# Turning q, k, v and the head output on VectorE and through DRAM scratch in place of TensorE

## The chip, the cores and the metric

The kernel runs on one core of a Trainium2 chip. The metric is the device time of one execution in microseconds (us), as the median of several executions. The engines named below are PE (TensorE, with its weight load PEld), DVE (VectorE), ACT (ScalarE), POOL (GpSimd) and SP (SyncE, which here issues nearly all DMAs).

## The reference

One layer of a hybrid decoder for a prompt of 1024 tokens (D_MODEL 1024, 8 heads of 128) and for 8 single tokens with stored states. Branch A is a gated delta rule, branch B a conformer convolution; both go through gates and an output projection, and a convolutional feed-forward layer follows. What the change touches is in branch A:

```python
qkv_c = jax.nn.silu(causal_dwconv(qkv, s_qkv, conv_qkv_w))
q, k = l2norm(q), l2norm(k)                       # per head, over 128 channels
...
def step(s, xc):                                   # scan over chunks, per head
    qg_c, kg_c, u_c, w_c, qk_c, gl_c = xc
    v_new = u_c - jnp.einsum('bhck,bhkv->bhcv', w_c, s)
    o = jnp.einsum('bhck,bhkv->bhcv', qg_c, s) + jnp.einsum('bhij,bhjv->bhiv', qk_c, v_new)
    s = s * gl_c[..., None, None] + jnp.einsum('bhck,bhcv->bhkv', kg_c, v_new)
    return s, o
...
o = o * lax.rsqrt(jnp.mean(o * o, axis=-1, keepdims=True) + NORM_EPS) * delta_norm_w
o = o * jax.nn.silu(z)
y_a = o.reshape(b, t, V_DIM) @ w_o_delta
```

All of it is float32. The kernel reaches that by splitting each operand of a large product into a high and a low part and running three products (`gemm`, line 187).

## The kernel before

The input projection is a sequence of weight tiles of 128 output columns. Each weight tile is multiplied with the activations in three column tiles of 344 tokens; `gemm` issues 24 products of 128x344 for one of them, into one of two PSUM buffers `mm`. Raw weights come by SP into `wraw` (two buffers, line 144), ACT casts them to `whi` (L145), DVE or POOL makes `wlo` (L146). Per head there are tiles for k, q, v (`qkv_tile`: ACT evicts, DVE adds the short convolution with three `scalar_tensor_tensor`), for z, and gate and conformer tiles between them. The outputs `kT`, `qT`, `vT`, `zT` hold channels on partitions and 1024 tokens along the row.

The head work runs in the gaps of these products. It is written as Python generators that `tick` (L157) advances once in four products of a gemm (L189); `yield n` lets 2n ticks pass. The order of PE is exactly the order in which the program writes it (`manual_schedule`, L89). DVE, ACT, POOL and SP each have an order that a list scheduler set when the kernel was built; on the chip each engine runs its own list in order and waits where an operand is missing. A head's stages are:

- `delta_a` (L638): products of k with itself, their masks, and the solve of 32x32 blocks on DVE, with two small turns through DRAM (`d_a` to `ab`, `d_x` to `dt`, L688 to L711).
- `delta_q` (L716): products of k with q, and the sums of squares of q per token. For these `sumsq` (L626) turns q with eight 128x128 PE transposes (L631), and ACT squares the PSUM tiles (L635).
- `delta_b` (L740): v and k are turned in the same way (L753), and ACT scales them into `vs` and `kt` (L756). Then the blocks of the solve are merged: DVE puts `dt` into `xs` (L770, a 32x32 stream transpose), PE begins with the products of L773. Then comes the chain over 8 chunks of 128 tokens (L814 to L842). One step is: PE `pk` (L817), DVE `vs` (L82), PE `pv` (L822), ACT `vn` (L825), PE `po` (L828), PE `psS` (L831), DVE `S` (L82, or L837 in the first step), PE `po` again (L838), ACT twice into `oo` (L840, L841). The PSUM tags of `pk`/`pv`, `po` and `psS` have one buffer each.
- `delta_c` (L847): ACT scales `oo` per token (L860); in four quarters PE turns two chunks (L867) and DVE multiplies with `dnw` and `zT` back into `oo` (shown as L82, since `stt` is a helper). SP stores `oo` to `d_og` (L875), from which the heads come back as `og` later. The last head skips the store and is split in place into `oghi`/`oglo`, which the product with `wod` reads next.

`oo`, `kt`, `vs`, `zT` have one buffer each, so the chain of head h+1 can write its first `oo` (L840) only when head h's `oo` is stored (L875). In parallel DVE works off the depthwise convolution of the conformer (`cacc`, 240 instructions of 128x512).

Of the kernel before, what the change touches and what calls it, by code (L numbers as in the profile page):

```python
# [8 lines left out]
F32 = mybir.dt.float32  # L9
F32R = mybir.dt.float32r  # L10
I32 = mybir.dt.int32
AF = mybir.ActivationFunctionType
ALU = mybir.AluOpType
# [3 lines left out]
P = 128  # L17
D = 1024
KT = D // P
T = 1024  # L20
# [4 lines left out]
NH = 8  # L25
NC = T // P
HB = 32
# [39 lines left out]
def body(tc, I, O):  # L67
    nc = tc.nc
# [9 lines left out]
    def sub(out, a, b):  # L78
        nc.vector.tensor_tensor(out=out, in0=a, in1=b, op=ALU.subtract)  # L79

    def stt(out, a, s, b, op0, op1):
        nc.vector.scalar_tensor_tensor(out=out, in0=a, scalar=s, in1=b, op0=op0, op1=op1)  # L82

    def split(hi, lo, x):
        nc.scalar.copy(hi, x)  # L85
        sub(lo, x, hi.bitcast(F32))

    with top:
        top.enter_context(tc.manual_schedule(engines={mybir.EngineType.PE}))  # L89
        dram = top.enter_context(tc.tile_pool(name="dram", bufs=1, space=DRAM))  # L90
# [7 lines left out]
        ident = const[:, C_ID:C_ID + P]  # L98
# [9 lines left out]
        def rsqrt(out, x, pool, shape, iters=3):  # L108
            t = pool.tile(shape, F32, tag="rs_t", name="rs_t")
            nc.vector.tensor_scalar(out=out.bitcast(I32), in0=x.bitcast(I32), scalar1=-0.5, scalar2=MAGIC,  # L110
                                    op0=ALU.mult, op1=ALU.add)
            for _ in range(iters):
                mul(t, out, out)
                stt(t, t, -0.5, x, ALU.mult, ALU.mult)
                stt(out, t, 1.5, out, ALU.add, ALU.mult)
# [116 lines left out]
        dnw = cp.tile([P, 1], F32, name="dnw")  # L232
# [28 lines left out]
        hp = hstk.enter_context(tc.tile_pool(name="hp", bufs=1, side="right", **R))  # L261
# [8 lines left out]
        def trp():  # L270
            return pst.tile([P, 512], F32, tag="tr", name="tr")
# [351 lines left out]

        cs = [slice(c * P, (c + 1) * P) for c in range(NC)]

        def sumsq(src, ss):  # L626
            for half in range(2):
                g = trp()
                gv = g.rearrange("p (c i) -> p c i", i=P)
                for i in range(4):  # L630
                    nc.tensor.transpose(gv[:, i, :], src[:, cs[half * 4 + i]], ident)  # L631
                for i in range(4):
                    c = half * 4 + i
                    jk = hp.tile([P, P], F32, tag="jk", name="jk")
                    nc.scalar.activation(jk, gv[:, i, :], AF.Square, accum_out=ss[:, c:c + 1])  # L635
                yield 2

        def delta_a(X):  # L638
            h, kT = X["h"], X["kT"]
# [76 lines left out]
        def delta_q(X):  # L716
            h, kT, qT = X["h"], X["kT"], X["qT"]
            while "sc" not in X:
                yield
            pt = X["pt"]  # L720
            brk, c1, nc1g, rqs = X["sc"]
            gr2 = hp.tile([P, NC, P], F32, tag="gr", name="gr2")
            nc.sync.dma_start(gr2.rearrange("p c i -> p (c i)"),
                              d_gc[1, h * NC:(h + 1) * NC].rearrange("c i -> (c i)").unsqueeze(0).broadcast_to([P, T]))
            yield 3
            for half in range(2):
                g = trp()
                gv = g.rearrange("p (c i) -> p c i", i=P)
                for i in range(4):
                    c = half * 4 + i  # L730
                    nc.tensor.matmul(gv[:, i, :], kT[:, cs[c]], qT[:, cs[c]], start=True, stop=True)  # L731
                mul(pt[:, 4 * half:4 * half + 4, :], gv, pt[:, 4 * half:4 * half + 4, :])
                yield
            ss = hp.tile([P, NC], F32, tag="ss", name="ss")
            yield from sumsq(qT, ss)
            nc.vector.tensor_scalar(out=rqs, in0=ss, scalar1=EPS, scalar2=EPS / QS ** 2, op0=ALU.add, op1=ALU.mult)
            mul(qT, qT, gr2.rearrange("p c i -> p (c i)"))
            X.update(qdone=True)

        def delta_b(X):  # L740
            h, kT, qT, vT = X["h"], X["kT"], X["qT"], X["vT"]
# [4 lines left out]
            kt = hp.tile([P, NC, P], F32, tag="kt", name="kt")  # L746
            vs = hp.tile([P, NC, P], F32, tag="vs", name="vs")
            for src, dst, scl in ((vT, vs, brk), (kT, kt, eg[:, h, :])):
                for half in range(2):
                    g = trp()  # L750
                    gv = g.rearrange("p (c i) -> p c i", i=P)
                    for i in range(4):
                        nc.tensor.transpose(gv[:, i, :], src[:, cs[half * 4 + i]], ident)  # L753
                    for i in range(4):
                        c = half * 4 + i
                        nc.scalar.activation(dst[:, c, :], gv[:, i, :], AF.Copy, scale=scl[:, c:c + 1])  # L756
                    yield
                X["vt"] = True
            while "dt" not in X:
                yield  # L760
# [5 lines left out]
            zv = zp[:, 0:256].rearrange("p (c i) -> p c i", i=HB)  # L766
# [12 lines left out]
            tv = tp_[:, 0:256].rearrange("p (c i) -> p c i", i=HB)  # L779
# [32 lines left out]
            oo = hp.tile([P, NC, P], F32, tag="oo", name="oo")  # L812
# [30 lines left out]
            nc.sync.dma_start(O["dp"][:, h, :], S)  # L843
            X.update(oo=oo, ms=ms, chained=True)
            X["fin"] = spawn(delta_c(X))

        def delta_c(X):  # L847
            h, oo, ms, rqs = X["h"], X["oo"], X["ms"], X["sc"][3]
            while h == NH - 1 and oglo[h] is None:
                yield  # L850
            f = hp.tile([P, NC], F32, tag="f", name="f", bufs=2)
            x = hp.tile([P, NC], F32, tag="fx", name="fx")
            stt(x, ms, 1.0 / P, rqs, ALU.mult, ALU.add)
            rsqrt(f, x, hp, [P, NC])
            yield 6
            while "zT" not in X:
                yield
            zT = X["zT"]
            for c in range(NC):
                nc.scalar.activation(oo[:, c, :], oo[:, c, :], AF.Copy, scale=f[:, c:c + 1])  # L860
            yield 2
            for qr in range(4):
                g = trp()[:, 0:256]
                gv = g.rearrange("p (c i) -> p c i", i=P)
                for i in range(2):
                    c = qr * 2 + i
                    nc.tensor.transpose(gv[:, i, :], oo[:, c, :], ident)  # L867
                og = oo[:, 2 * qr:2 * qr + 2, :].rearrange("p c i -> p (c i)")
                sl = slice(256 * qr, 256 * qr + 256)
                stt(og, g, dnw, zT[:, sl], ALU.mult, ALU.mult)  # L870
                if h == NH - 1:
                    split(oghi[h][:, sl], oglo[h][:, sl], og)
                yield
            if h < NH - 1:
                nc.sync.dma_start(d_og[h], oo.rearrange("p c i -> p (c i)"))  # L875
            X["done"] = True
# [74 lines left out]
        oghi, oglo = [None] * NH, [None] * NH  # L951
# [32 lines left out]
        def chain_b():  # L984
            for h in range(NH):
                while len(Xs) <= h:
                    yield
                yield from delta_b(Xs[h])
# [128 lines left out]
        for m in range(KT):  # L1117
            w = next_w()
            for t, (t0, n, npr) in enumerate(th):
                sg = sgp.tile([P, TH], F32, tag="sg", name="sgb")  # L1120
                nc.sync.dma_start(sg, d_gb[m, :, t0:t0 + TH])
                g, bufs = sas[(NTH * m + t) % 4]
# [169 lines left out]
        for b in range(2):  # L1292
            X[b] = xpool[b].tile([P, KT, HB2], F32, name=f"x{b}")
            for m in range(KT):
# [13 lines left out]
                for j in range(2):  # L1308
                    sl = slice(j * Q, j * Q + Q)
# [419 lines left out]
```

## Time and profile before

| what | value |
|---|---|
| median of 3 executions | 1832.4 us (1830.82 to 1833.6) |
| the profiled execution | 1833.88 us, its span 1832.1 us |
| mean granted TensorE clock | 0.995 of full speed |
| busy: PE / PEld | 1792.0 us (98%) / 1769.3 us (97%) |
| busy: DVE / ACT / POOL | 1377.5 us (75%) / 892.7 us (49%) / 127.7 us (7%) |
| DMA queue of SP | 37.0% of 16 engines' span |

Busy time counts the instructions of an engine; PE's products are pipelined, so the distance of two starts, and not the duration of one, tells what an instruction adds. Heads 0 to 7 occupy 60 to 870 us of the span, about 91 us for each; output projection and feed-forward follow and are not touched by the change.

### The profile page before, as it was taken

How to read it: one execution, taken by the hardware profiler on the slowest of the kernel's cores; microseconds unless marked ns; L12 is line 12 of the kernel's file. 1: busy time of each engine (PE TensorE's matmuls, PEld its weight loads, DVE VectorE, ACT ScalarE, POOL GpSimd, SP SyncE). 2: the span in 40 equal slices, each digit the busy share in tenths (PEclk: the TensorE clock that was granted, in tenths of full speed). 3: DMA queues.
4: the chain of work that ended last, by engine and by line, in shares of the span. 5: the costliest groups of instructions: out<-in, count | busy, mean ns of one | idle time of the engine just before them, and what ended most of it. 6: DMA issues, size and time to landing. Idle time of an engine off the chain costs nothing.

```text
span 1832.1 us, 35468 instructions
## 1 busy us (share of the span) xinstructions
PE 1792.0 (98%) x13331; PEld 1769.3 (97%) x13331; DVE 1377.5 (75%) x3266; ACT 892.7 (49%) x2112; POOL 127.7 (7%) x249
## 2 busy tenths in 40 slices
PE   7899999999999999999999998999999999999997
PEld 6899999999999999999999998999999999999997
DVE  7998799689967996745438488987888788856553
ACT  5565466455655555554213344544444445544332
POOL 4410010001000100000000000100000000000000
PEclk9999999999999999999999999999999999999998
DMA  4143323222323233334657632322222224867562
GB/s 165 55 137 99 92 73 114 88 85 82 115 86 86 81 122 99 105 135 131 191 158 223 224 127 93 103 70 92 73 79 75 87 76 150 259 204 215 168 185 85
DMA packets 150988, 223.83 MB, mean 122 GB/s; under 512 B 37984, under 2 KB 86432, under 8 KB 150816
## 3 DMA queue, kind: packets, MB, share of 16 engines
q1 hardware_dynamic: 143760, 213.10, 37.0%
q10 hardware_dynamic: 7056, 8.47, 1.3%
q8 instruction: 104, 1.70, 0.4%
q14 instruction: 68, 0.56, 0.1%
HBM read 172.36 MB, written 49.14 MB: 121 GB/s over the span
## 4 chain that ended last, share of the span: by engine, by line
PE 91%; DVE 5%; DMA 2%; ACT 1%; issue 1%; SPq 0%; DVEq 0%; ACTq 0%
PE mm L187 44%; PE mm L1333 23%; PE mm L1598 13%; PE psS L831 1%; PE tr L666 1%; PE tr L731 1%; PE tr L753 1%; PE po L838 1%; PE pv L822 1%; PE po L828 1%; PE pk L817 1%; DVE xt L82 1%; PE tr L794 0%; PE tr L804 0%; PE tr L908 0%
## 5 line engine op out<-in xcount | busy, mean ns | idle before, releaser
L187 PE MATMUL mm<-hhi,whi 128*128 128x344 f32 x1360 | 449.3, 330 | 12.4 <-ACT whi L85 6.9
L187 PE MATMUL mm<-hhi,wlo 128*128 128x344 f32 x1360 | 448.4, 330 | 2.5 <-DVE wlo L79 2.4
L187 PE MATMUL mm<-hlo,whi 128*128 128x344 f32 x1360 | 438.5, 328 | 0.0
L187 PEld LDWEIGHTS mm<-hhi,whi 128*128 128x128 f32 x1360 | 258.4, 190 | 16.5 <-ACT whi L85 7.3
L187 PEld LDWEIGHTS mm<-hhi,wlo 128*128 128x128 f32 x1360 | 258.5, 190 | 4.8 <-DVE wlo L79 3.7
L187 PEld LDWEIGHTS mm<-hlo,whi 128*128 128x128 f32 x1360 | 254.9, 188 | 0.5
L1333 PE MATMUL mm<-l_t,uhi 128*128 128x258 f32 x704 | 200.3, 285 | 1.4 <-DVE l_t L79 1.4
L1333 PE MATMUL mm<-h_t,uhi 128*128 128x258 f32 x704 | 200.4, 285 | 0.0
L1333 PE MATMUL mm<-h_t,ulo 128*128 128x258 f32 x704 | 199.3, 283 | 0.0
L82 DVE SCALAR_TENSOR_TENSOR cacc<-u,ccw,cacc 128x512 f32<-128x512 f32 x240 | 172.6, 742 | 1.0 <-ACT cacc L570 0.9
L1598 PE MATMUL mm<-yl,wdh 128*128 128x344 f32 x528 | 169.5, 321 | 0.0
L1598 PE MATMUL mm<-yh,wdh 128*128 128x344 f32 x528 | 169.5, 321 | 0.0
L1598 PE MATMUL mm<-yh,wdl 128*128 128x344 f32 x528 | 169.3, 321 | 0.0
L79 DVE TENSOR_TENSOR wdl<-draw,wdh 128x512 fp32r<-128x512 f32 x144 | 91.9, 645 | 82.2 <-ACT wdh L85 80.6
L145 ACT CAST whi<-wraw 128x512 fp32r<-128x512 f32 x164 | 96.5, 628 | 100.9 <-PE mm L187 82.8
L85 ACT CAST wdh<-draw 128x512 fp32r<-128x512 f32 x144 | 82.9, 584 | 114.9 <-PE mm L1598 99.6
L1333 PEld LDWEIGHTS mm<-l_t,uhi 128*128 128x128 f32 x704 | 133.8, 190 | 2.2 <-DVE l_t L79 2.2
L1333 PEld LDWEIGHTS mm<-h_t,uhi 128*128 128x128 f32 x704 | 133.7, 190 | 0.5 <-ACT h_t L1190 0.2
L1333 PEld LDWEIGHTS mm<-h_t,ulo 128*128 128x128 f32 x704 | 133.5, 190 | 0.0
L187 PE MATMUL mm<-og,whi 128*128 128x344 f32 x512 | 123.1, 321 | 0.0
L146 DVE TENSOR_TENSOR wlo<-wraw,whi 128x512 fp32r<-128x512 f32 x160 | 107.9, 689 | 14.7 <-ACT whi L145 12.1
L85 ACT CAST uhi<-s 128x512 fp32r<-128x512 f32 x92 | 56.9, 621 | 105.3 <-PE mm L1333 101.4
(358 smaller groups left out, 4228.8 us busy)
## 6 DMA issues: line engine op xcount, KB each, us to landing
draw<-in_wdn SPq DMA_DIRECT2D x120, 256.0 KB, 2.8
raw<-in_wup SPq DMA_DIRECT2D x92, 256.0 KB, 2.7
yl<-d_y SPq DMA_DIRECT2D x21, 516.0 KB, 6.0
d_y<-av SPq DMA_DIRECT2D x21, 512.0 KB, 3.2
gr<-d_gc SPq DMA_DIRECT2D x16, 512.0 KB, 3.4
wraw<-in_wout SPq DMA_DIRECT2D x32, 256.0 KB, 2.8
xt<-in_xT SPq DMA_DIRECT2D x12, 344.0 KB, 6.7
d_ga<-sg ACTq DMA_DIRECT2D x24, 172.0 KB, 2.4
```

Source lines behind the costliest of these rows:

```text
L79: nc.vector.tensor_tensor(out=out, in0=a, in1=b, op=ALU.subtract)
L82: nc.vector.scalar_tensor_tensor(out=out, in0=a, scalar=s, in1=b, op0=op0, op1=op1)
L85: nc.scalar.copy(hi, x)
L145: nc.scalar.copy(hi[:, k:k + 4], raw)
L146: weng["e"].tensor_tensor(out=lo[:, k:k + 4], in0=raw, in1=hi[:, k:k + 4].bitcast(F32), op=ALU.subtract)
L187: nc.tensor.matmul(ps, lhs[:, k, :], r(k), start=k == 0 and i == 0, stop=k == kt - 1 and i == 2)
L666: nc.tensor.matmul(gv[:, i, :], kT[:, cs[c]], kT[:, cs[c]], start=True, stop=True)
L731: nc.tensor.matmul(gv[:, i, :], kT[:, cs[c]], qT[:, cs[c]], start=True, stop=True)
L753: nc.tensor.transpose(gv[:, i, :], src[:, cs[half * 4 + i]], ident)
L817: nc.tensor.matmul(pk, kT[:, cs[c]], S, start=True, stop=True)
L1333: nc.tensor.matmul(z[:, b, 0:Q], w[:, k, :], r[b][nm][:, k, :], start=start and n == 0, stop=n == 3 * KH - 1, skip_group_check=True)
L1598: nc.tensor.matmul(ps, w[:, f % KH, :], y[:, f % 3, :], start=h == 0 and n == 0, stop=h == 1 and n == 3 * (NF - 3 * KH) - 1)
```

## The change

A helper `flip` turns a 128x1024 tile: DVE transposes its 32x32 blocks in one STREAM_TRANSPOSE into `ty`, SP stores `ty` to DRAM scratch `d_t` (512 KB, two buffers), and four SP loads of 128 KB each bring it back with the blocks in their transposed places, into `tv`. `ty` and `tv` have the same tag with one buffer, so the load overwrites what was stored, and the next flip begins when the readers of `tv` are done. Each head has four flips: q for `sumsq`, v and k in `delta_b`, `oo` in `delta_c`. ACT and DVE read `tv` in SBUF where they read PSUM before. The waits between the stages, in ticks, change with it: 3 in place of 2 and 2 for q, 2 and 2 in place of 1, 1, 1, 1 for v and k, 2 and 1 in place of four times 1 for `oo`.

```diff
--- before.py
+++ after.py
@@ -623,17 +623,24 @@
 
         cs = [slice(c * P, (c + 1) * P) for c in range(NC)]
 
+        def flip(src):
+            ty = hp.tile([P, T], F32, tag="ty", name="ty")
+            d_t = dram.tile([P, T], F32, tag="d_t", name="d_t", bufs=2)
+            nc.vector.transpose(out=ty, in_=src.rearrange("p (c b r) -> p b c r", b=4, r=HB))
+            nc.sync.dma_start(d_t, ty)
+            tv = hp.tile([P, T], F32, tag="ty", name="tv")
+            dv = d_t.rearrange("(a r) (b x) -> b r a x", r=HB, b=4)
+            for b in range(4):
+                nc.sync.dma_start(tv[HB * b:HB * (b + 1)].rearrange("p (a x) -> p a x", a=4), dv[b])
+            return tv.rearrange("p (a c s) -> p c a s", a=4, c=NC)
+
         def sumsq(src, ss):
-            for half in range(2):
-                g = trp()
-                gv = g.rearrange("p (c i) -> p c i", i=P)
-                for i in range(4):
-                    nc.tensor.transpose(gv[:, i, :], src[:, cs[half * 4 + i]], ident)
-                for i in range(4):
-                    c = half * 4 + i
-                    jk = hp.tile([P, P], F32, tag="jk", name="jk")
-                    nc.scalar.activation(jk, gv[:, i, :], AF.Square, accum_out=ss[:, c:c + 1])
-                yield 2
+            tv = flip(src)
+            yield 3
+            for c in range(NC):
+                jk = hp.tile([P, P], F32, tag="jk", name="jk")
+                nc.scalar.activation(jk.rearrange("p (a s) -> p a s", a=4), tv[:, c], AF.Square,
+                                     accum_out=ss[:, c:c + 1])
 
         def delta_a(X):
             h, kT = X["h"], X["kT"]
@@ -746,15 +753,11 @@
             kt = hp.tile([P, NC, P], F32, tag="kt", name="kt")
             vs = hp.tile([P, NC, P], F32, tag="vs", name="vs")
             for src, dst, scl in ((vT, vs, brk), (kT, kt, eg[:, h, :])):
-                for half in range(2):
-                    g = trp()
-                    gv = g.rearrange("p (c i) -> p c i", i=P)
-                    for i in range(4):
-                        nc.tensor.transpose(gv[:, i, :], src[:, cs[half * 4 + i]], ident)
-                    for i in range(4):
-                        c = half * 4 + i
-                        nc.scalar.activation(dst[:, c, :], gv[:, i, :], AF.Copy, scale=scl[:, c:c + 1])
-                    yield
+                tv = flip(src)
+                yield 2
+                for c in range(NC):
+                    nc.scalar.activation(dst[:, c, :].rearrange("p (a s) -> p a s", a=4), tv[:, c], AF.Copy,
+                                         scale=scl[:, c:c + 1])
                 X["vt"] = True
             while "dt" not in X:
                 yield
@@ -859,18 +862,16 @@
             for c in range(NC):
                 nc.scalar.activation(oo[:, c, :], oo[:, c, :], AF.Copy, scale=f[:, c:c + 1])
             yield 2
-            for qr in range(4):
-                g = trp()[:, 0:256]
-                gv = g.rearrange("p (c i) -> p c i", i=P)
-                for i in range(2):
-                    c = qr * 2 + i
-                    nc.tensor.transpose(gv[:, i, :], oo[:, c, :], ident)
-                og = oo[:, 2 * qr:2 * qr + 2, :].rearrange("p c i -> p (c i)")
-                sl = slice(256 * qr, 256 * qr + 256)
-                stt(og, g, dnw, zT[:, sl], ALU.mult, ALU.mult)
-                if h == NH - 1:
-                    split(oghi[h][:, sl], oglo[h][:, sl], og)
-                yield
+            tv = flip(oo.rearrange("p c i -> p (c i)"))
+            yield 2
+            zv, ov = zT.rearrange("p (c b r) -> p b c r", b=4, r=HB), oo.rearrange("p c (b r) -> p b c r", b=4)
+            for b in range(4):
+                stt(ov[:, b], tv[:, :, b], dnw, zv[:, b], ALU.mult, ALU.mult)
+            if h == NH - 1:
+                og = oo.rearrange("p c i -> p (c i)")
+                for o in (0, 512):
+                    split(oghi[h][:, o:o + 512], oglo[h][:, o:o + 512], og[:, o:o + 512])
+            yield
             if h < NH - 1:
                 nc.sync.dma_start(d_og[h], oo.rearrange("p c i -> p (c i)"))
             X["done"] = True
```

The change adds 32 STREAM_TRANSPOSE to DVE, takes the 256 transposes from PE (11336 rows to 11255 with their grouping), and takes SP from 540 to 622 rows. The rest of PE's products keep their order.

How the lists move, at two places. First DVE around the beginning of the chain of head 1. `S<-psS` is the state after its first chunk, the next `vs<-` and `S<-S` are the second chunk's steps, `cacc` the conformer's convolution, `oo<-` the end of head 0. Before:

```order
L82 SCALAR_TENSOR_TENSOR oo<-tr,dnw,zT 128x256
L73 TENSOR_TENSOR prd<-stq,cqw 128x32
L82 SCALAR_TENSOR_TENSOR cacc<-u,ccw,cacc 128x512
L837 COPY S<-psS 128x128
L82 SCALAR_TENSOR_TENSOR qT<-raw,cqw,qT 128x344
L82 SCALAR_TENSOR_TENSOR cacc<-u,ccw,cacc 128x512
L82 SCALAR_TENSOR_TENSOR qT<-raw,cqw,qT 128x344
L82 SCALAR_TENSOR_TENSOR cacc<-u,ccw,cacc 128x512
L82 SCALAR_TENSOR_TENSOR vs<-pk,sc,vs 128x128
L82 SCALAR_TENSOR_TENSOR qT<-raw,cqw,qT 128x344
L82 SCALAR_TENSOR_TENSOR cacc<-u,ccw,cacc 128x512 x3
L82 SCALAR_TENSOR_TENSOR qT<-raw,cqw,qT 128x344
```

After `cacc` once more stands `S<-S`. With the change the same stretch, from the second chunk's `vs` to its `S`, on DVE:

```order
L82 SCALAR_TENSOR_TENSOR vs<-pk,sc,vs 128x128
L82 SCALAR_TENSOR_TENSOR qT<-raw,cqw,qT 128x344
L82 SCALAR_TENSOR_TENSOR cacc<-u,ccw,cacc 128x512
L82 SCALAR_TENSOR_TENSOR qT<-raw,cqw,qT 128x344
L82 SCALAR_TENSOR_TENSOR cacc<-u,ccw,cacc 128x512 x6
L82 SCALAR_TENSOR_TENSOR oo<-tv,dnw,zT 128x8x32 x4
L82 SCALAR_TENSOR_TENSOR cacc<-u,ccw,cacc 128x512 x11
L82 SCALAR_TENSOR_TENSOR qT<-raw,cqw,qT 128x344
L82 SCALAR_TENSOR_TENSOR S<-S,gl,psS 128x128
```

The end of head 0's `oo` has moved from ahead of the chain to between the two steps of its second chunk, and 18 `cacc` now stand between these where 4 stood. The flip's transpose of this `oo` stands six rows ahead of `S<-psS`. In head 7's chain the four `oo<-tv` stand at the same place, right behind the second chunk's `vs`, and in heads 2 to 6 ahead of its first step.

Second, the queue of SP around the solve of head 4, whose `dt` is read back from `d_x`. `d_vn`, `vb`, `out_ds` and `Sb` belong to the decode tokens, `d_t` and `tv` in the lower list to the flip of head 3's `oo`. Before:

```order
L708 DMA d_x<-xr 32x8x32 x4
L711 DMA dt<-d_x 32x256 x4
L144 DMA wraw<-in_wz 128x512 x2
L922 DMA d_vn<-vr 8x128
L924 DMA vb<-d_vn 128x1024
L875 DMA d_og<-oo 128x1024
```

With the change:

```order
L715 DMA d_x<-xr 32x8x32 x4
L925 DMA vb<-d_vn 128x1024
L630 DMA d_t<-ty 128x1024
L718 DMA dt<-d_x 32x256 x4
L634 DMA tv<-d_t 32x4x256 x4
L144 DMA wraw<-in_wb 128x512
L144 DMA wraw<-in_wa 128x512
L932 DMA out_ds<-Sb 128x1024
```

The loads of `dt` stand behind the store of the flip now, and two 512 KB transfers lie between the two halves of the solve's turn. Head 6 has the same row order there.

## Rows read from the trace of the kernel before

**Rows 1.** Page of the profile: busy time by engine, and the shares of the span of the chain that ended last, by engine.

```profile
PE 1792.0 (98%) x13331; PEld 1769.3 (97%) x13331; DVE 1377.5 (75%) x3266; ACT 892.7 (49%) x2112; POOL 127.7 (7%) x249
...
PE 91%; DVE 5%; DMA 2%; ACT 1%; issue 1%; SPq 0%; DVEq 0%; ACTq 0%
```

**Rows 2.** Busy time by stretch of 100 us: start:end and length, then busy us (instructions) of PE, PEld, DVE, ACT, POOL, then granted clock, DMA share, GB/s.

```profile
400.00:500.00 100.00, 100.00 (x765) 98.57 (x764) 96.18 (x274) 58.06 (x174) 8.07 (x15) 1.00 0.32 103
500.00:600.00 100.00, 99.71 (x761) 97.98 (x760) 72.27 (x250) 59.86 (x183) 5.30 (x18) 1.00 0.27 80
```

**Rows 3.** Timeline of PE around one group of four transposes of q: start us, duration us, engine, line, operation, tile.

```profile
111.18 0.32 PE L187 MATMUL mm<-hhi,wlo 128*128 128x344 f32 x1
111.34 0.60 PE L631 MATMUL tr<-const,qT 128*128 128x128 f32 x4
111.70 0.41 PE L187 MATMUL mm<-hlo,whi 128*128 128x344 f32 x1
111.94 0.32 PE L187 MATMUL mm<-hhi,whi 128*128 128x344 f32 x1
```

**Rows 4.** Timeline of PE around one group of two transposes of `oo`.

```profile
512.56 0.32 PE L187 MATMUL mm<-hhi,wlo 128*128 128x344 f32 x1
512.72 0.38 PE L867 MATMUL tr<-const,oo 128*128 128x128 f32 x2
512.86 0.40 PE L187 MATMUL mm<-hlo,whi 128*128 128x344 f32 x1
513.10 0.32 PE L187 MATMUL mm<-hhi,whi 128*128 128x344 f32 x1
```

**Rows 5.** Groups of instructions on PE: line, engine, operation, tile, shape and count, then busy us, mean ns of one, and idle time before them.

```profile
L867 PE MATMUL tr<-const,oo 128*128 128x128 f32 x64 | 12.1, 273 | 0.0
L753 PE MATMUL tr<-const,vT 128*128 128x128 f32 x64 | 9.6, 272 | 0.0
L631 PE MATMUL tr<-const,qT 128*128 128x128 f32 x64 | 9.6, 272 | 0.0
L753 PE MATMUL tr<-const,kT 128*128 128x128 f32 x64 | 9.6, 272 | 0.0
```

**Rows 6.** Groups of instructions on DVE, the same columns.

```profile
L82 DVE SCALAR_TENSOR_TENSOR oo<-tr,dnw,zT 128x256 f32<-128x256 f32 x32 | 15.3, 477 | 4.6 <-PE tr L867 4.5
...
L73 DVE TENSOR_TENSOR pt<-am,const 128x1024 f32<-128x1024 f32 x8 | 9.7, 1215 | 0.0
```

**Rows 7.** The stream transposes that the kernel has already: count, then ns of one (shortest/median/longest), first and last start.

```profile
L770 DVE STREAM_TRANSPOSE xs<-dt x8: 437/442/446, 175.8 to 773.7; 128x256 f32<-128x256 f32 x8
```

**Rows 8.** DMA issues: what, queue, operation and count, KB each, median us from issue to landing.

```profile
d_y<-av SPq DMA_DIRECT2D x21, 512.0 KB, 3.2
...
gr<-d_gc SPq DMA_DIRECT2D x16, 512.0 KB, 3.4
...
ab<-d_a SPq DMA_DIRECT2D x32, 128.0 KB, 3.7
```

**Rows 9.** Timeline of SP's issues, at 121 us and at 256 us.

```profile
121.25 0.80 SPq L692 DMA_DIRECT2D ab<-d_a  x2
...
256.55 0.33 SPq L875 DMA_DIRECT2D d_og<-oo  x1
```

**Rows 10.** Timeline of DVE in the chain of head 1, from the second chunk's `vs` to its `S`, cut.

```profile
259.84 0.35 DVE L82 SCALAR_TENSOR_TENSOR vs<-pk,sc,vs 128x128 f32<-128x128 f32 x1
260.10 0.57 DVE L82 SCALAR_TENSOR_TENSOR qT<-raw,cqw,qT 128x344 f32<-128x344 f32 x1
260.59 2.07 DVE L82 SCALAR_TENSOR_TENSOR cacc<-u,ccw,cacc 128x512 f32<-128x512 f32 x3
...
263.73 0.34 DVE L82 SCALAR_TENSOR_TENSOR S<-S,gl,psS 128x128 f32<-128x128 f32 x1
```

**Rows 11.** Timeline of ACT there: the first chunk's `oo`.

```profile
260.21 0.28 ACT L840 ACTIVATE oo<-po 128x128 f32<-128x128 f32 x1 [2.77 <-DVE vs L82]
...
260.61 0.27 ACT L841 COPY oo<-po 128x128 f32<-128x128 f32 x1
```

**Rows 12.** Timeline of PE in the chains of head 1 (261 us) and head 7 (810 us): the second chunk's product with the state.

```profile
261.35 0.39 PE L828 MATMUL po<-S,qT 128*128 128x128 f32 x2
...
810.02 0.39 PE L828 MATMUL po<-S,qT 128*128 128x128 f32 x2
```

**Rows 13.** Timeline of DVE: the second chunk's `vs` in head 7's chain.

```profile
808.12 0.35 DVE L82 SCALAR_TENSOR_TENSOR vs<-pk,sc,vs 128x128 f32<-128x128 f32 x1
```

**Rows 14.** Timeline of ACT: the last scaled chunks of head 7's `oo`.

```profile
862.18 0.69 ACT L860 ACTIVATE oo<-oo,f 128x128 f32<-128x128 f32 x2
```

**Rows 15.** Timeline of PE: the beginning of the product with `wod`.

```profile
869.84 0.40 PE L187 MATMUL mm<-og,whi 128*128 128x344 f32 x1
```

**Rows 16.** Timeline of DVE: `xs` of head 4.

```profile
511.26 0.45 DVE L770 STREAM_TRANSPOSE xs<-dt 128x256 f32<-128x256 f32 x1
```

**Rows 17.** Timeline of PE: the first products of head 4's merge.

```profile
523.13 0.69 PE L773 MATMUL tr<-dt,am 32*32 32x32 f32 x32
```

**Rows 18.** Busy time by stretch of 10 us after the heads, columns as in the second group.

```profile
1110.00:1120.00 10.00, 7.41 (x62) 7.16 (x60) 8.53 (x28) 3.77 (x8) 0.65 (x1) 0.99 0.27 95
1120.00:1130.00 10.00, 10.00 (x72) 9.76 (x72) 7.86 (x14) 3.47 (x7) 0.62 (x2) 0.84 0.15 51
```

**Rows 19.** What SP's queue waited for: line, what, us in total, times, longest us.

```profile
SPq L144 <- DVE wlo L146: 168.2, 83, 13.4
```

## The prediction, made before the changed kernel ran

> **What bounds the kernel now.** I read the page first: its busy times and its chain that ended last. PE is busy 98% of the span and holds 91% of that chain; DVE, second, holds 5% [rows 1]. The reader should see that nothing but the length of PE's own list, and the few places where PE waits, sets the time: a microsecond of path taken from PE is a microsecond gained, unless PE then waits for something. Then the busy times by stretch, since the 75% of DVE are a mean: from 400 to 500 us DVE is busy for 96.18 us, from 500 to 600 us for 72.27 us, PE for 100.00 and 99.71 us [rows 2]. DVE has slack, but not in each head. Last I read the timelines at the four places where the built order of the changed kernel puts something late in front of PE.
>
> The profiled execution took 1833.88 us, 1.5 us more than the median of 1832.4 us. I make the sum against the former and take 1.5 us off at the end. A difference under 0.2%, 3.7 us, can't be told from none here.
>
> **What PE gets back.** A transpose shows a duration of 272 ns [rows 5], but PE is pipelined, and only starts count. Around a group of four, a product starts at 111.18 and the second one after it at 111.94 us [rows 3]: 0.76 us, where two distances of 0.157 us (111.34 less 111.18) would be 0.31. A group of four costs 0.45 us. A group of two costs 513.10 less 512.56, less 0.31, so 0.23 us [rows 4]. There are 192 transposes of q, v, k in groups of four and 64 of `oo` in groups of two [rows 5]: 48 x 0.45 + 32 x 0.225 = **28.8 us less on PE**. The ends, were the distances read 10% wrong, are 26 and 32 us. By the durations it would be 40.9 us; the starts decide.
>
> The Trainium skill (VectorE: DVE Perf Modes, The three transpose paths, and Rules for kernel authors) gives 390 ns for a 128x128 transpose on TensorE in another type and advises TensorE wherever a PSUM destination will do, which speaks against this change. By its figure PE would get back 100 us and the sum below would be near -77 us; by the starts it is 28.8 us, and the starts are of this kernel.
>
> **What a flip costs.** DVE: the one stream transpose in the trace has 128x256 elements and takes 442 ns [rows 7]; four times that is 1.77 us, and an operation on 128x1024 takes 1.215 us [rows 6]. I take 1.22 us, since that row has the same size, and keep 1.77 for the range. The 32 flips put 39 us (to 57) on DVE, 4.9 us in each head of 91 us. The store is like the other 512 KB stores, 3.2 us [rows 8]. The loads are 128 KB each like `ab`, 3.7 us to landing [rows 8], and SP issues them 0.40 us apart [rows 9], so the last lands 3 x 0.40 + 3.7 = 4.9 us after the first issue. One flip is 1.2 + 3.2 + 4.9 = **9.3 us** before anyone can read it, where a PE transpose could be read at once; at the worst, behind two weight loads, I give it 15 us. SP's 160 new issues lie on a queue with slack; the four loads wait there for the store, and weight loads stand behind them, which costs nothing so long as the three prepared weight tiles last.
>
> For q, v and k the result is due tens of microseconds later, at the chain, so PE waits for none of these 24 flips: zero, under the condition of the second rival. ACT reads SBUF where it read PSUM, 64 instructions each: no change that PE sees. The four `stt` per `oo` have as many elements as before, 0.48 us each [rows 6], starting 0.40 apart.
>
> **Where PE waits instead.** `oo` is the tight one, because the next head's chain may write it only when it is stored.
>
> *Head 1.* DVE has `oo<-tv` behind the second chunk's `vs`, which ended its turn at 260.10 us in the trace of before [rows 10]. Between the two stand, in the new list, two `qT` of 0.49 us (260.10 to 260.59) and seven `cacc` of 0.66 (three take 2.07 less the overlap of one start, 1.98): 5.6 us. So `oo<-tv` runs from 265.7 to 267.3, the store issues in 0.33 us [rows 9] and lands in 3.4 (as 512 KB do [rows 8]), and ACT writes the first chunk's `oo` 0.67 us [rows 11] after 271.0. The buffer `po` is free at 271.7 us; PE wanted it at 261.35 [rows 12]. **+10.4 us.** From the flip's own latency, which starts some 4.7 us ahead of `S<-psS`, the wait would be 7; a lower end of 5 if PE's lead carries DVE along, an upper of 12 from the 18 `cacc` ahead of `S`.
>
> *Head 7.* `oo<-tv` again stands right behind the second `vs`, whose turn is at 808.12 [rows 13]: from 808.4 to 810.0, store landed at 813.7, ACT's copies to 814.4, and PE wanted `po` at 810.02 [rows 12]. **+4.4 us** (0 to 6).
>
> *The end of head 7.* ACT scales the last `oo` until 862.9 us [rows 14]. With 9.3 for the flip, 1.6 for four `stt` and 1.9 for the split (ACT 0.6, DVE twice 0.65) it is ready at 875.7. The product with `wod` began at 869.84 [rows 15] and comes to head 7's part after 21 products of 0.157 us, at 873.1, less 0.9 us of transposes that no longer stand ahead of it: 872.2. **+3.5 us** (1 to 6).
>
> *Heads 4 and 6.* `xs` was ready at 511.26 us [rows 16], and PE took the merge up at 523.13 [rows 17]. Now `dt` is loaded behind the flip's store, and `xs` stands on DVE behind the last `kT` and `oo`'s transpose. The 12 us of slack are about used up: between 0 and the 3.4 us of one transfer, I take 1.5 each, **+3.0 us**. In heads 2, 3 and 5 `oo<-tv` stands ahead of the first chunk and costs nothing; up to 1 us each in the range.
>
> *The clock.* After a stretch in which PE was busy for 7.41 of 10 us, the next 10 us show a granted clock of 0.84 [rows 18], so 1.6 us lost. The wait of head 1 is long enough for one such dip, **+1.6 us**; the others I leave at zero, to 3 us in the range.
>
> Sum: -28.8 + 10.4 + 4.4 + 3.5 + 3.0 + 1.6 = -5.9 us, so 1828.0 us for a profiled execution and **1826.5 us** for the median. The gain on PE is sure; what eats it is less so, so this case's own range is 1819 to 1834.
>
> **The rivals.** *First, the waits vanish.* The scheduled places come out earlier as PE's lead grows, DVE's idle 28 us between 500 and 600 us [rows 2] speaks for it, and only head 1 and the end still wait, some 7 us together: -28.8 + 7 on 1832.4 is 1811 us. Against it: DVE's and SP's lists are in a fixed order, and head 1's stands in it as told.
>
> *Second, slower: ACT waits in order for late flips.* The built lists hold a flip's readers at fixed places on ACT. Where the four loads come late, ACT stands, and behind it the evictions of `mm`. PE has one more buffer: 24 products of 0.157 us, 3.8 us of cover. In many heads the four loads stand on SP behind weight loads, which in the kernel before waited 168.2 us in all for `wlo` to free their buffer, up to 13.4 us at a time [rows 19]. A flip then takes 15 us and not 9.3, and ACT holds PE for 5.7 less 3.8, about 2 us, and with each such wait DVE's `vs` and `S` come later as well. If 12 of the 24 flips of q, v and k do so, that is 24 us: 1826.5 + 24 is about 1850 us. It decides against the change from 0.25 us on average in each of the 24 (5.9 / 24). For it: `ty` is one buffer that also holds up the next flip, so lateness is passed on. Against it: in the built order the readers stand about one flip behind, and SP's queue has 37% use.
>
> *Third, DVE becomes the bound in the full heads.* From 400 to 500 us, 96.2 + 4.9 us of DVE work must fit into 100 less 3.6 us of PE: 4.7 us late there, and about as much in one other head: 1826.5 + 9 is 1835 us. Against it: `cacc` can be late, and the wait in head 1 gives DVE time.
>
> **How the numbers follow.** Forecast 0.40 (0.29 faster, 0.09 same, 0.02 slower, by its own range); waits vanish 0.15, all faster; ACT waits 0.30, all slower; DVE the bound 0.15 (0.06 same, 0.09 slower). Together faster 0.44, same 0.15, slower 0.41. The range reaches a little past the first rival's 1811 us and the second's 1850, to 1809 and 1853, and leaves out about a third of the first and four tenths of the second, 0.17 in all.
>
> **What would show it.** PE's busy time is not the test, since it falls by the durations; the distance of starts is. Head 1's chain should show PE waiting about 10 us ahead of the second chunk's `po`, head 7's 4, the product with `wod` 3. The flips should land 9 to 10 us after their stream transpose, at about 1.2 us each. I am wrong if PE waits several microseconds for ACT's evictions beside the flips of q, v and k, if DVE's transposes take 1.7 us or more, or if head 1 shows no wait.

## The result and the profile after

| | median us | runs from to | ratio to before, 95% interval |
|---|---|---|---|
| before | 1833.0 | 1830.82 to 1834.67 | |
| with the change | 1851.04 | 1848.84 to 1853.36 | 1.0101 (1.0088 to 1.0113) |

The change makes the kernel slower by 1.0%, 18 us, where 6 us faster was forecast. The profiled execution's span is 1851.5 us against 1832.1, so 19.4 us more, and its mean granted clock 0.984 against 0.995.

The page of the changed kernel, first its busy times, then the flips' DMAs (KB each, median us to landing):

```profile
PE 1778.0 (96%) x13075; PEld 1753.3 (95%) x13075; DVE 1408.7 (76%) x3296; ACT 895.8 (48%) x2110; POOL 123.9 (7%) x249
...
d_t<-ty SPq DMA_DIRECT2D x32, 512.0 KB, 2.9
tv<-d_t SPq DMA_DIRECT2D x128, 128.0 KB, 3.0
```

Against [rows 1], PE's busy time fell by 14 us while the span grew by 19: PE's idle time went from 40 to 73 us. DVE has 31 us more. The store of a flip lands after 2.9 us (3.2 was taken), a load after 3.0 (3.7).

What PE waited for, by line (us in total, times, longest). None of these four rows has a counterpart of any size before:

```profile
PE tr L776 <- DMA dt<-d_x: 15.4, 5, 8.6
PE po L831 <- ACT oo L844: 9.9, 2, 9.0
...
PE mm L187 <- ACT og L85: 3.0, 1, 3.0
...
PE mm L187 <- ACT zT L529: 2.5, 1, 2.5
```

That is 30.8 us. Where it happened, in PE's timeline (the bracket is the idle time and its releaser):

```profile
179.32 0.31 PE L776 MATMUL tr<-dt,am 32*32 32x32 f32 x2 [8.57 <-DMA dt<-d_x]
...
274.92 0.79 PE L831 MATMUL po<-S,qT 128*128 128x128 f32 x2 [8.98 <-ACT oo L844]
...
531.63 0.24 PE L776 MATMUL tr<-dt,am 32*32 32x32 f32 x2 [1.30 <-DMA dt<-d_x]
...
712.69 1.02 PE L776 MATMUL tr<-dt,am 32*32 32x32 f32 x20 [4.90 <-DMA dt<-d_x]
...
888.66 0.43 PE L187 MATMUL mm<-og,whi 128*128 128x344 f32 x1 [2.97 <-ACT og L85]
```

Head 0's merge waits 8.57 us for `dt`, head 1's second chunk 8.98 us for `oo`, head 4's and head 6's merge 1.30 and 4.90 us for `dt`, the product with `wod` 2.97 us.

The clock, in stretches around three of these waits (length, then busy us of PE, PEld, DVE, ACT, POOL, then the granted clock, DMA share, GB/s). A granted clock of 1.00 is the higher of its two levels (2.4 GHz) throughout, 0.50 would be the lower (1.2 GHz); a value between is a mix of both:

```profile
170.00:180.00 10.00, 1.07 (x7) 0.65 (x5) 8.07 (x37) 3.19 (x10) 0.40 (x1) 0.80 0.46 151
180.00:190.00 10.00, 9.97 (x103) 9.19 (x104) 2.47 (x5) 2.87 (x7) 0.29 (x2) 0.69 0.56 133
260.00:270.00 10.00, 5.95 (x41) 5.75 (x39) 9.94 (x20) 2.17 (x6) 0.33 (x1) 0.91 0.39 107
270.00:280.00 10.00, 5.08 (x24) 5.08 (x25) 10.00 (x19) 2.17 (x8) 1.78 (x1) 0.58 0.13 52
...
265.90:274.90 9.00, 0.04 (x1) 0.00 (x0) 9.00 (x17) 1.29 (x5) 0.00 (x0) 0.63 0.14 59
274.90:280.00 5.10, 5.08 (x24) 5.08 (x25) 5.10 (x10) 1.53 (x5) 1.78 (x1) 0.66 0.00 0
712.70:720.00 7.30, 7.27 (x83) 6.72 (x84) 4.76 (x15) 2.83 (x9) 0.19 (x1) 0.59 0.71 216
```

After PE was busy for 1.07 of 10 us, it ran at a granted clock of 0.69 for the next 10; behind the wait of head 1 at 0.66 up to 280 us; behind head 6's at 0.59 up to 720 us. An estimate of what the clock takes is its shortfall times PE's busy time in the stretch: 0.2 + 3.1 us, 1.7 and 3.0 us here (from 260 to 270 us nothing, since the shortfall there lies in the wait, where PE had no work), and with the stretches at 60, 810, 820 and 890 us (0.83, 0.88, 0.94, 0.86) some 13 us in all. The one at 60 us, 1.7, stands ahead of every flip, so 11 us go with the new waits. In the kernel before no such stretch from 60 to 920 us is below 0.98.

So the balance is about -27 us of transposes (below), +31 us of waits, +13 us of clock: +17 of the 19.4.

### The profile page after: what moved, and what is told of

It is laid out like the page before. It is cut to its first block, busy times and chain, and to the rows that moved or that the text cites. A ratio compares the mean times of both kernels' runs of the same rounds, so it can differ in the third digit from the quotient of the medians.

```text
span 1851.5 us, 35290 instructions
## 1 busy us (share of the span) xinstructions
PE 1778.0 (96%) x13075; PEld 1753.3 (95%) x13075; DVE 1408.7 (76%) x3296; ACT 895.8 (48%) x2110; POOL 123.9 (7%) x249
## 3 DMA queue, kind: packets, MB, share of 16 engines
q1 hardware_dynamic: 166800, 246.66, 42.7%
## 4 chain that ended last, share of the span: by engine, by line
PE 64%; DVE 4%; DMA 3%; ACT 2%; issue 1%; SPq 0%; DVEq 0%; ACTq 0%
PE mm L1334 23%; PE mm L187 23%; PE mm L1599 13%; DMA wraw<-in_wout 0%; PE psS L834 0%; DVE l_t L79 0%; PE nrm_b L224 0%; PE po L841 0%; PE pv L825 0%; DMA d_ch<-c 0%; DMA dt<-d_x 0%; PE pk L820 0%; PE po L831 0%; ACT whi L145 0%; PE tr L673 0%
## 5 line engine op out<-in xcount | busy, mean ns | idle before, releaser
L187 PE MATMUL mm<-hhi,whi 128*128 128x344 f32 x1360 | 450.6, 331 | 13.6 <-ACT whi L85 6.7
L146 DVE TENSOR_TENSOR wlo<-wraw,whi 128x512 fp32r<-128x512 f32 x160 | 108.2, 689 | 16.4 <-ACT whi L145 15.4
```

The costliest lines, as they stand in the source:

```text
L146: weng["e"].tensor_tensor(out=lo[:, k:k + 4], in0=raw, in1=hi[:, k:k + 4].bitcast(F32), op=ALU.subtract)
L187: nc.tensor.matmul(ps, lhs[:, k, :], r(k), start=k == 0 and i == 0, stop=k == kt - 1 and i == 2)
```

## The experiments

The rival theories after the comparison were: **L**, the latency of the turn through DRAM and the one buffer `ty`; **D**, the time of the stream transposes on an already full DVE; **P**, that PE's transposes cost little before. All ratios are to runs of the kernel before on the same chip.

| run | what | median us | ratio (95%) |
|---|---|---|---|
| no_turn | no transposes of any kind | 1810.5 | 0.9887 (0.9871 to 0.9904) |
| no_stream | turn through DRAM without stream transposes | 1822.7 | 0.9946 (0.9931 to 0.9961) |
| no_dram | stream transposes without the turn | 1845.8 | 1.0076 (1.0060 to 1.0092) |
| oo_own_buffer | second buffer for flips of `oo` | 1851.0 | 1.0102 (1.0087 to 1.0117) |
| fewer_taps | 64 of 240 `cacc` left out | 1829.8 | 0.9979 (0.9968 to 0.9989) |
| oo_on_pe | flips of q, v, k only | 1823.8 | 0.9948 (0.9933 to 0.9963) |
| oo_only | flips of `oo` only | 1834.9 | 1.0010 (1.0000 to 1.0021) |
| q_only | flips of q only | 1831.4 | 0.9991 (0.9981 to 1.0000) |
| qkv_1_7 | flips of q, v, k in heads 1 to 7 | 1822.4 | 0.9942 (0.9927 to 0.9957) |
| h0_on_pe | the change, head 0's q, v, k on PE | 1845.6 | 1.0066 (1.0051 to 1.0081) |
| oo0_on_pe | the change, head 0's `oo` on PE | 1840.4 | 1.0043 (1.0029 to 1.0057) |
| plain_op | a plain operation for each stream transpose | 1851.4 | 1.0096 (1.0076 to 1.0116) |

**no_turn** makes `flip` return its source:

```diff
-            ty = hp.tile(...) ... nc.vector.transpose(...) ... 4 loads into tv
-            return tv.rearrange("p (a c s) -> p c a s", a=4, c=NC)
+            return src.rearrange("p (a c s) -> p c a s", a=4, c=NC)
...
-                stt(ov[:, b], tv[:, :, b], dnw, zv[:, b], ALU.mult, ALU.mult)
+                stt(ov[:, b], ov[:, b], dnw, zv[:, b], ALU.mult, ALU.mult)
```

> Leaves out the turning of q, k, v and oo altogether (readers take the tile as it stands; oo is multiplied in place): no PE transposes, no stream transposes, no turn through DRAM. It prices what PE gets back. Theory L (the changed kernel loses by the latency of the turn and its one buffer) and theory D (it loses by the 39 us of stream transposes on a full DVE) both expect 28.8 us less than before, about 1804 us (1800 to 1812). Theory P (PE transposes lay in gaps, the starts were misread) expects 1825 us or more.

Measured 1810.5 us, 21.7 us (1.13%) less than before. P falls. The size is best read between two merges that no wait disturbs, head 3's and head 7's first products, in PE's timeline of before and of no_turn:

```profile
431.23 0.69 PE L773 MATMUL tr<-dt,am 32*32 32x32 f32 x32
...
786.72 0.69 PE L773 MATMUL tr<-dt,am 32*32 32x32 f32 x32
```

```profile
421.90 0.69 PE L768 MATMUL tr<-dt,am 32*32 32x32 f32 x32
...
763.79 0.69 PE L768 MATMUL tr<-dt,am 32*32 32x32 f32 x32
```

355.5 us against 341.9: 13.6 us in four heads, 3.4 us a head or 27 us in eight, where the prediction had 3.6 and 28.8. The term was right within 6%; the 5 us between 27 and 22 are not accounted for one by one.

**no_stream** and **no_dram** take the two halves of a flip apart:

```diff
 no_stream
-            ty = hp.tile([P, T], F32, tag="ty", name="ty")
-            nc.vector.transpose(out=ty, in_=src.rearrange(...))
-            nc.sync.dma_start(d_t, ty)
+            nc.sync.dma_start(d_t, src)
 no_dram
-            nc.sync.dma_start(d_t, ty)
-            tv = hp.tile(...); dv = ...; for b in range(4): nc.sync.dma_start(...)
+            tv = ty
```

> Leaves out the 32x32 transposes on DVE (SP stores the tile itself); the turn through DRAM, its store, its four loads and its one buffer stay. Theory L: 1843 us or more, since every transfer and buffer is still there; the waits for dt and for oo in the changed kernel (25 us with the clock behind them) remain. Theory D: the solve of heads 0, 4 and 6 gets its DVE time back, the wait for dt (15.4 us) goes, and the time falls to 1835 us or less.

> Leaves out the turn through DRAM (readers take ty as DVE wrote it, so blocks stay in their places); the 32 stream transposes stay. Theory L: close to no_turn, 1804 to 1815 us, and no wait of PE for oo in head 1. Theory D: DVE is as full as in the changed kernel, the solve is late, PE waits for dt in heads 0, 4, 6: 1825 us or more.

With no_turn and the change they make a square. Without stream transposes: 1810.5 without, 1822.7 us with the turn. With them: 1845.8 and 1851.0 us. The stream transposes cost 35 us where the turn is out and 28 us where it is in; the turn costs 12 and 5 us. Both times that D expected hold, those of L fail. What PE waited for, in no_stream and then in no_dram:

```profile
PE tr L774 <- DMA dt<-d_x: 3.8, 2, 3.2
PE po L829 <- ACT oo L842: 3.7, 1, 3.7
```

```profile
PE tr L771 <- DMA dt<-d_x: 26.9, 8, 7.6
```

Without the turn PE waits 26.9 us for `dt`, and not at all for `oo`; without the stream transposes the wait for `dt` is 3.8 us. So the wait for `dt` goes with DVE's time, though `dt` comes by DMA and no flip is among what it is made from. The 3.2 us that are left of it in no_stream lie in head 0, where no_turn has 1.4 too. One part of L's expectation did hold: the wait of head 1 for `oo` is gone in no_dram, and it is 3.7 us in no_stream, so its 8.98 us need both halves of the flip.

**plain_op** asks whether it is the stream transpose as such:

```diff
-            nc.vector.transpose(out=ty, in_=src.rearrange("p (c b r) -> p b c r", b=4, r=HB))
+            add(ty, src, src)
```

> Each stream transpose replaced by one plain two-operand operation of the same 128x1024 on DVE (about 1.22 us, so blocks are not turned); all else as in the changed kernel. If DVE's time is what counts: 1851 us within 5. If the stream transpose as such disturbs (ports, drains, the place the list gives it): 1835 us or less, near no_stream's 1823.

1851.4 us, and the same waits (in the profiled execution, which was the shortest of four, 1845.3 us). It is DVE's time, not the kind of operation:

```profile
PE tr L776 <- DMA dt<-d_x: 15.1, 4, 8.6
PE po L831 <- ACT oo L844: 9.9, 2, 9.0
```

**fewer_taps** keeps all flips and lightens DVE elsewhere:

```diff
                 for o in (0, 512):
-                    stt(acc[:, o:o + 512], u[:, j + o:j + o + 512], ...)
+                    if j % 4:
+                        stt(acc[:, o:o + 512], u[:, j + o:j + o + 512], ...)
                     yield 1.5
```

> The changed kernel with 8 of the 30 convolution taps left out on DVE (64 of 240 cacc, 42 us at a distance of 0.66 us); ticks, flips, transfers and buffers as in the changed kernel. The runs so far name theory D (DVE is full, and while cacc are left over the list puts them between the dependent steps of the solve, so heads 0, 4, 6 deliver dt late): the solve of heads 4 and 6 falls from 31 to 25 us or less, the wait for dt from 15.4 to 4 us or less, the time to 1830 us or less, about 1825. Theory L (the turn through DRAM and its buffer): 1843 us or more.

1829.8 us, 21 us less than the change (42 us of DVE left out; before would gain from that too, which wasn't run). PE waits for `dt` nowhere; the wait for `oo` of head 1 stays in full:

```profile
PE po L832 <- ACT oo L845: 9.5, 1, 9.5
```

So there are two losses, and leaving out taps mends the first alone: in its head 1 seven `cacc` still stand between the second chunk's `vs` and `oo<-tv`. The first loss can be seen on DVE in the solve of head 4, 31 dependent pairs `xt`, `xx` between the first `xt` and the copy `xr`. Before:

```profile
480.47 0.21 DVE L73 TENSOR_TENSOR xt<-ab,xx 128x31 f32<-128x31 f32 x1
...
486.54 0.20 DVE L73 TENSOR_TENSOR xt<-ab,xx 128x52 f32<-128x52 f32 x1
486.77 0.22 DVE L79 TENSOR_TENSOR xx<-xx,xt 128x52 f32<-128x52 f32 x1
487.02 0.22 DVE L73 TENSOR_TENSOR xt<-ab,xx 128x50 f32<-128x50 f32 x1
...
501.88 0.40 DVE L706 COPY xr<-xx 128x256 f32<-128x256 f32 x1
```

With the change:

```profile
491.98 0.22 DVE L73 TENSOR_TENSOR xt<-ab,xx 128x31 f32<-128x31 f32 x1
...
500.17 0.21 DVE L73 TENSOR_TENSOR xt<-ab,xx 128x52 f32<-128x52 f32 x1
500.29 0.75 DVE L82 SCALAR_TENSOR_TENSOR cacc<-u,ccw,cacc 128x512 f32<-128x512 f32 x1
500.95 0.22 DVE L79 TENSOR_TENSOR xx<-xx,xt 128x52 f32<-128x52 f32 x1
501.08 0.75 DVE L82 SCALAR_TENSOR_TENSOR cacc<-u,ccw,cacc 128x512 f32<-128x512 f32 x1
...
523.48 0.41 DVE L713 COPY xr<-xx 128x256 f32<-128x256 f32 x1
```

Before, 21.4 us, and 3 `cacc` lie in it; now 31.5 us and 13 `cacc`. In head 6 it is 23.8 us with 4 and 32.8 us with 14, in head 0 32.6 and 39.1 us. In the odd heads no `cacc` lies in it, and it takes 17 to 21 us in both. The flips ahead of it push convolution work back: when head 4's solve begins, 177 of the 240 `cacc` are done before and 167 with the change. In a part of the solve the built list then puts one `cacc` of 0.66 us between each two dependent steps, whose turn comes each 0.25 us otherwise. In fewer_taps head 4's solve takes 18.1 us and head 6's 20.8.

A long solve alone does not make PE wait. In oo_on_pe (below) the solves of heads 4 and 6 take 29.3 and 33.1 us with 12 and 13 `cacc`, and PE waits 0 and 1.5 us for their `dt`: it comes to the merge 39.9 and 40.2 us after the solve's start there, 38.4 and 36.5 us in the changed kernel, 42.7 us for both before. So the solve of heads 4 and 6 is late by its length and by its start. A list that keeps `cacc` out of the solve was not run, so whether the order alone would save the time is open.

**oo_own_buffer** lets the flips of `oo` of heads 0 to 5 use the idle buffer of `ab`:

```diff
-            tv = flip(oo.rearrange("p c i -> p (c i)"))
+            tv = flip(oo.rearrange("p c i -> p (c i)"), "ab" if h < NH - 2 else "ty")
```

> The changed kernel, with the flips of oo of heads 0 to 5 in the buffer of the solve's ab, which is idle then, so that the flip of oo need not wait until ACT has read the next head's k from the one buffer. Theory L with the one buffer as the cause: the wait of 9 us for oo in head 1 shrinks by the 3 to 6 us that the flip of oo starts earlier, the dip of the clock behind it with it: 1838 to 1845 us. If the buffer is not the cause: 1851 us within 3.

The median is the change's, as was expected if the buffer is not the cause. But in the profiles the wait for `oo` falls from 9.9 to 4.3 us, and the one for `dt` rises from 15.4 to 18.5:

```profile
PE tr L776 <- DMA dt<-d_x: 18.5, 6, 8.6
...
PE po L831 <- ACT oo L844: 4.3, 2, 3.4
```

What stands behind the wait of head 1 can be read in its rows, first ACT's and DVE's in the changed kernel, then DVE's in oo_own_buffer:

```profile
253.27 2.45 ACT L759 ACTIVATE kt<-tv,eg 128x128 f32<-128x128 f32 x8
```

```profile
256.18 1.25 DVE L629 STREAM_TRANSPOSE ty<-oo 128x1024 f32<-128x1024 f32 x1
...
263.93 0.35 DVE L82 SCALAR_TENSOR_TENSOR vs<-pk,sc,vs 128x128 f32<-128x128 f32 x1
...
265.83 4.06 DVE L82 SCALAR_TENSOR_TENSOR cacc<-u,ccw,cacc 128x512 f32<-128x512 f32 x6
269.80 0.48 DVE L82 SCALAR_TENSOR_TENSOR oo<-tv,dnw,zT 128x256 f32<-128x256 f32 x1
...
349.88 1.25 DVE L629 STREAM_TRANSPOSE ty<-oo 128x1024 f32<-128x1024 f32 x1 [2.91 <-ACT kt L759]
```

```profile
249.46 1.25 DVE L629 STREAM_TRANSPOSE ty<-oo 128x1024 f32<-128x1024 f32 x1 [0.52 <-ACT oo L863]
...
263.46 1.66 DVE L82 SCALAR_TENSOR_TENSOR oo<-tv,dnw,zT 128x256 f32<-128x256 f32 x4
```

ACT reads the next head's k out of `tv` until 255.7 us, and `oo` is turned at 256.18, but DVE did not stand idle for it: it came there from other work. DVE stood for ACT's readers of the one buffer in heads 1 and 6, 2.91 and 3.46 us (349.88 us above, and 802.35). The last load of the flip is issued at 262.5 us and lands 3.1 us later, and six `cacc` then hold `oo<-tv` back for some 4 us more, without idle time of DVE either. With its own buffer the flip starts 6.7 us earlier, and in the list built for it no `cacc` stands between the second chunk's `vs` and `oo<-tv`; the wait is 3.40 us. In no_stream no `cacc` stands there either, and it is 3.74. So the wait of head 1 is the flip's lateness and the `cacc` ahead of `oo<-tv` together, and no run parts the two in full. That mending it would pay is not shown.

**oo0_on_pe** puts head 0's `oo` alone back on PE (`if h == 0:` the four quarters of before, `else:` the flip).

> The changed kernel with head 0's oo alone on PE; the other 31 flips stay. The wait of 9.0 us of head 1 for oo goes, with the dip behind it (granted clock 0.91 and 0.58 in the 20 us from 260 us, 5 us): 1851 - 9 - 5 + 1, about 1838 us (1833 to 1842). If the wait is not that turn's: 1848 us or more.

1840.4 us: 10.6 less than the change, for one flip of 32. The wait and the dip are gone; the stretches of 10 us at 260 and 270 us have PE busy for all of them, at full clock:

```profile
260.00:270.00 10.00, 10.00 (x70) 10.00 (x69) 9.78 (x21) 4.18 (x14) 2.96 (x2) 1.00 0.31 105
270.00:280.00 10.00, 10.00 (x74) 10.00 (x73) 9.75 (x32) 4.76 (x13) 0.48 (x3) 1.00 0.20 69
```

**h0_on_pe** puts head 0's q, v and k back on PE in the same manner.

> The changed kernel with head 0's q, v, k on PE; the other 29 flips stay. The same wait of 8.6 us goes, with its dip: 1851 - 8.6 - 5 + 2.7, about 1840 us (1835 to 1844), the wait of head 1 for oo (9 us) stays. If the waits only move on: 1848 us or more.

1845.6 us, 5.4 less than the change, where 11 were expected. The wait of 8.57 us is gone. The 5 us that I gave to the clock were too many: of the stretch at 170 to 180 us, with a clock of 0.80, PE used 1 us. Nor did the clock come back with the wait: by the same estimate 11.8 us go to it from 60 to 920 us in this run, 13.2 in the changed kernel, among them a stretch at 180 us that stays at 0.83 with PE busy for 8.79 of 10 us. The wait of head 1 for `oo` grew to 9.5 us.

**oo_on_pe**, **oo_only** and **q_only** take the flips by kind, with the code of before for the rest.

> Flips for q, v, k only (24); oo on PE as before. 7.2 us come back on PE, 10 us leave DVE. The wait of 9 us in head 1 with the clock's dip behind it (5 us) and the 3 us at the end with theirs go, the waits for dt mostly stay: 1851 + 7 - 20, about 1838 us (1833 to 1843) by theory D. If the flips of oo were harmless: 1855 us or more.

> Flips for oo only (8); q, v, k on PE as before. PE gets 7.2 us back, DVE 10 us more, 1.2 us a head. Theory D: little backlog, solve of heads 4 and 6 at 21 to 26 us, no wait for dt over 3 us; the turn of oo still waits at head 1 (up to 5) and at the end (3 and its dip): 1832 - 7 + 11, about 1836 us (1830 to 1842). Theory L with oo as the tight one: the losses of head 1 and the end in full, 1843 us or more.

> Flips for q only (8); v, k, oo on PE. PE gets 7.2 us back, DVE 10 us more; q is due late, so the turn's latency can't be waited for. Theory D with 10 us a small backlog: wait for dt up to 4 us: 1825 to 1830 us, faster than before. If any flip costs more than it gives: 1833 us or more.

1823.8, 1834.9 and 1831.4 us. oo_only came as theory D expected; oo_on_pe came out faster than either expectation, and q_only between the two. The 24 flips of q, v and k gain 0.5%, the 8 of `oo` cost 0.1% (just at the edge), and both together cost 1.0%: some 26 us lie in their meeting. It is seen at head 1: alone the flip of `oo` makes PE wait 3.3 us there, without a `cacc` between `vs` and `oo<-tv`; behind the flip of k, and with seven, 8.98. And in oo_on_pe almost all of the wait for `dt` is head 0's 8.54 us:

```profile
PE tr L776 <- DMA dt<-d_x: 10.6, 3, 8.5
```

My 1838 us for it was too high by 14: it left the later waits for `dt` of heads 4 and 6 in (one of 1.5 us in head 6 remains over 0.6), the 2.5 us of `zT`, and the clock's dips at 710, 810 and 820 us that went with the flips of `oo`.

**qkv_1_7** joins oo_on_pe with h0_on_pe.

> Flips of q, v, k in heads 1 to 7 (21); head 0's q, v, k and all oo on PE. oo_on_pe kept one long wait, 8.5 us for dt of head 0 with a clock of 0.95 from 100 to 200 us (5 us) behind it. By theory D head 0's solve, in the stretch with the most cacc, gets its time back: 1823.8 - 8.5 - 5 + 2.7 for the 24 transposes back on PE, about 1813 us (1808 to 1818). If that wait only moves to the next head: 1820 us or more.

1822.4 us: the fastest complete version, 0.6% under before, not told apart from oo_on_pe by its interval. The expectation of 1813 fails. The wait of head 0 did go and did not move on; one wait for `dt` is left:

```profile
PE tr L799 <- DMA dt<-d_x: 1.6, 1, 1.6
```

At head 7's merge qkv_1_7 is 5.8 us ahead of oo_on_pe (773.42 against 779.25 us), about the 8.5 of the wait less 2.7 for the transposes, with the clock's 5 us not found; of these 5.8, 1.7 are left at the end of the span. Where the other 4 went, behind the last flip, is open.

## Why the prediction was wrong

- **What bounds the kernel**: right. What PE gets back, 28.8 us: 27 by the undisturbed stretch, 22 by the median of no_turn. The starts, not the durations (40.9), were the right reading.
- **The price of a flip**: right for each part. DVE takes 1.24 us (1.22 was taken); count, then shortest/median/longest ns:

```profile
L629 DVE STREAM_TRANSPOSE ty<-oo x8: 1234/1245/1255, 256.2 to 875.8; 128x1024 f32<-128x1024 f32 x8
```

  The shortest time from a flip's start to its first reader is 10.4 us (9.3 was taken).
- **"For q, v and k ... PE waits for none of these 24 flips: zero"**: this step failed. No reader of q, v or k made PE wait, but the flips took DVE's time from the solve, which isn't their reader. Head 0's merge waited 8.57 us, taken at zero. The prediction read the slack of head 4, 12 us; head 0 had hardly any, as the trace of before shows:

```profile
168.28 1.71 SPq L711 DMA_DIRECT2D dt<-d_x  x4
...
173.46 0.69 PE L773 MATMUL tr<-dt,am 32*32 32x32 f32 x32
```

  The last of these four loads was issued at 169.6 us, a load of `dt` lands 2.6 us after its issue, and PE took the merge up at 173.46: 1.3 us of slack. With the change PE came 2.7 us earlier, as its transposes were gone (in no_turn, without any flip, it waits 1.4 us there), and the solve ended at 172.1 instead of 164.6 us. The 39 us were priced as if DVE's idle time could hold them; DVE is at 96.28 us of 100 from 400 to 500 us, as in [rows 2], so nothing was left there, and work moved into the stretch behind (some of the 9 us more there comes from the heads, which lie some 10 us later):

```profile
400.00:500.00 100.00, 99.12 (x747) 97.53 (x746) 96.28 (x277) 60.89 (x180) 7.41 (x16) 1.00 0.46 141
500.00:600.00 100.00, 97.48 (x732) 95.40 (x731) 81.36 (x286) 58.62 (x176) 5.11 (x19) 1.00 0.44 136
```

- **Heads 4 and 6**: 3.0 us were taken, 1.30 and 4.90 measured. The cause that I gave, `dt` behind the flip's store on SP, is not the main one: in no_dram there is no such store, and heads 2, 4 and 6 wait 5.1, 6.1 and 6.8 us. From the issue of `d_x` to that of the last load of `dt` it takes 6.3 and 5.2 us in heads 4 and 6, 4.5 and 4.4 before; the solve grew by 10.1 and 9.0 us.
- **Head 1**: right, 10.4 us taken, 8.98 measured, at the `po` named and by the rows named: 5.6 us of DVE's list between `vs` and `oo<-tv` (264.19 to 269.80 us), as taken. Head 7: 0.92 us at the second chunk and 2.51 where ACT couldn't evict z into `zT`, which `oo<-tv` read until 817.4 us; 3.4 where 4.4 was taken, in a way not foreseen; **the end**: 2.97 where 3.5 was taken.
- **"The clock ... the others I leave at zero"**: this step failed too. Head 1's dip was right, 1.6 us taken and 1.7 estimated from the rows; the others, taken at zero, come to some 9 us, about 11 in all. Each of the three waits of 4.9 us and more lies beside a stretch at 0.59 to 0.69.
- **The rivals**: the second rival's price, 1850 us, is what came, but not by its mechanism, so by luck: PE lists no wait for an eviction beside the flips of q, v and k. Nor did any of the three signs of being wrong appear: what failed was not among them. The third had the mechanism, DVE as the bound in the full heads, and excused it with "`cacc` can be late": they were, and it was the solve between them that paid. Its price of 9 us was too low. The Trainium skill's rule (VectorE: DVE Perf Modes, Rules for kernel authors) to keep 128x128 transposes on TensorE holds for the change as a whole, 1.0101; for q, v and k alone, 0.9948, the measurement decides against it.

In numbers: 1826.5, and 8.6 for head 0, 3.2 for heads 4 and 6, -1.4 and -1.0 for heads 1 and 7, -0.5 for the end, 9.4 for the clock gives 1844.8; the transposes' gain, smaller by 2 to 7 us, brings it to 1847 to 1852.

## What to carry to other kernels

Work that leaves a bound engine must be priced on the engine that takes it at its fullest stretch, and by who stands in the same list: here 1.24 us on DVE, 32 times, cost 28 to 35 us of the whole, since dependent small steps (the solve, and in head 1 the end of `oo`) had to share the list with a backlog of long independent ones. Move the pieces whose receiver has slack (q, v, k), leave those that sit in a dependence between two heads (`oo`). And price a new wait on PE together with the clock behind it: by the estimate above, 1.7 to 3.3 us for each of the three waits of 4.9 us and more in this trace.

## What the runs showed that was not expected

A stream transpose of 128x1024 costs 1.24 us, as much as a plain operation on two operands of that size (1.22), and less than four times the 0.442 us of one of 128x256 [rows 7]. The loads of 128 KB with runs of 1 KB from DRAM landed in 3.0 us in the median, sooner than `ab`'s 3.7 [rows 8].
